# A hybrid encoder layer with a mixture of experts: the first expert's rows by one-hot products, unread products beside the router, and the mix's slot later in the ring

## The chip, the cores and the metric

The kernel runs on one core of a Trainium2 chip. The metric is the device time of one execution in microseconds (us). The kernel before takes 1461.59 us, the median of three runs (1460.72 to 1464.11). The profiled execution took 1457.25 us; its span, from the first instruction to the last, is 1455.5 us.

Engines are named as in the profile: PE multiplies matrices (PEld loads its weights), DVE is the vector engine, ACT the scalar engine, POOL the general one; SP issues most of the transfers. A queue's own row (SPq, POOLq) is the instruction that issues or waits.

## The reference, cut to what matters

A sequence of 512 tokens of width 1024 goes through one layer. A gated linear recurrence and a sparse attention each give half of the mix; then the top 4 of 32 experts work on each token.

```
h  = rms_norm(x) * (1 + sc1) + sh1;  z = h @ w_in
y_rnn  = rg_lru(...)                      # 512 columns
y_attn = dsa_attention(q, k, v, ...)      # 8 heads of 64
mix = concat(rms_norm(y_rnn), rms_norm(y_attn)) @ w_out
x   = x + g1 * mix
h2  = rms_norm(x) * (1 + sc2) + sh2
logits = h2 @ w_router + b_router;  gates = softmax(top 4)
for each expert e, on the tokens that chose it:
    u   = h2[tok] @ w1[e] + b1[e]         # 1024 x 2048
    act = clamped_swiglu(u)
    y  += gate * (act @ w2[e] + b2[e])    # 1024 x 1024
out = x + g2 * y
```

All is fp32. The expert weights alone are 32 times 12 MB.

## The kernel before, in words

The tokens lie in four tiles of 128 (index `i`). After the input products and the recurrence the kernel forms the mix, `part` (four tiles of 1024 in SBUF at `R[6]`), which starts as x. `rg_out_half(i, n, ...)` (twelve products of 512 columns, written out by `mm3`) adds the recurrent half of the mix for one tile and one half of the columns; `mix_half` does so for the attention's half. Before, all eight `rg_out_half` are handed to `attend` in a list; `attend(i, between)` takes one of them after every second head. A scheduler then orders each engine's instructions by its own estimate of when they are ready, so an engine's order is not the program's; `order` rows below show it.

`norm_heads` and `prep_q` ready q for the heads. `router_tile(i)` transposes a finished tile of the mix, forms the router's logits, picks four experts (`selb`, 1 where chosen; `gts`, the gates), builds h2 for the tile and writes it to `h2_d` in HBM.

The experts come as places in a list: `ORDER` gives the number of 32-row blocks of each (`NBS`: 3, 3, then 4, 2, 3, 2, 3 five times, and 4, 2, 1, 2, 1). The first two places are experts 0 and 1, fixed; the other thirty are ranked by their number of rows (`rank_experts`). `places` computes for every token and expert the position among that expert's rows (`pos`); `route` turns positions into row numbers (`idx_all`) and gates by one-hot products; `gather` fetches the rows of h2 from HBM by an indirect DMA on POOL; `turn_x` transposes them on PE into `xTs`. Then `up` (8 weight blocks of 1 MB), `glu`, `turn_act`, `down` (4 blocks of 1 MB) and `add_out` (an indirect DMA that adds to the output). PE does up(j), then the transposes for j+1, then down(j-1). After the first `up`, `gated_bias` adds the experts' bias to `part` and writes it to the output as the base of the sums.

Weights arrive through a ring of nine slots of 16 KB per partition, two loads of 1 MB in each. `wslot` takes the slots in the order of `slots_at` and issues the two loads on SP, which works in order: a load that must wait for its slot holds up all later ones. The places `R[0]` to `R[6]` (16 KB each) and those at 148 and 164 have earlier uses, and a slot's first load waits for these: R1, weights of the recurrent half; 148 and 164, k and q; R2, R5, weights of the attention's half; R4, y; R3 and R0, work space of the router; R6, the mix, which is free only when `gated_bias` has written it out.

```
for j in range(E + 1):
    ...
        w = load_up(w1_of(expert(j)));  up(j, w, nb);  glu(j, nb)
        turn_x(j + 1, ...);  bias(j + 1, ...)
    if j == 0: gated_bias()
    if j: down(load_down(w2_of(expert(j - 1))), ...);  add_out(j - 1, ...)
```

Of the kernel before, what the change touches and what calls it, by code (L numbers as in the profile page):

```python
# [13 lines left out]
OP = mybir.AluOpType  # L14
# [5 lines left out]
NT = S // 128  # L20
KD = D // 128
# [16 lines left out]
def layer(ctx, tc, x, c, w_ada, b_ada, norm1_g, w_in, conv_w, conv_b, w_rg_a, b_rg_a, w_rg_x, b_rg_x,  # L38
# [74 lines left out]
    A2r, sh2r = [mem(R[3] + 8 + 4 * j, D) for j in range(2)]  # L113
# [432 lines left out]
    load_wo(1)  # L546
    rq = norm_heads(zq, "q", 191.5, [mem(174.75 + 2 * j, S) for j in range(2)])
# [77 lines left out]

    def router_tile(i):
        o = part[:, i]
        x2T, h2 = [mem(R[0] + 8 * j + 4 * (i % 2), D) for j in range(2)]
        x2T = x2T.rearrange("p (k t) -> p k t", k=KD)
        for q in range(2):  # L630
            p = bank(4, 5)
            for k in range(4):
                T.transpose(p[:, k * 128:(k + 1) * 128], o[:, 4 * q + k::KD], ident)
            A.copy(x2T[:, 4 * q:4 * q + 4, :], p.rearrange("p (k t) -> p k t", k=4))
        ss2 = const.tile([128, 1], F32, name="ss2", tag="ss2", bufs=2)
# [32 lines left out]
    rg = [partial(rg_out_half, i, n, *half_a) for i in (3, 2, 1, 0) for n in range(2)]  # L668
    attend(3, rg[0:4])
# [17 lines left out]
    attend(2, rg[4:6] + [partial(mix_half, 3, n, *m3, *half_b) for n in range(2)])  # L687
    m2 = mix_in(2)
    attend(1, rg[6:8] + [partial(mix_half, 2, n, *m2, *half_b) for n in range(2)])
# [35 lines left out]
    slots_at = (164, 148, R[1], R[4], R[2], R[5], R[0], R[3], R[6])  # L725
# [91 lines left out]
    def wslot(blocks, n, src):  # L817
        nslot[0] += 1
        kb = slots_at[(nslot[0] - 1) % len(slots_at)]
        t = [mem(kb + 8 * j, blocks, n) for j in range(2)]  # L820
        for j in range(2):
            nc.sync.dma_start(t[j], src(j))
        return t
# [33 lines left out]
    def turn_x(j, frm, nb):  # L857
        n = BT * (4 if nb == 3 else nb)
        for q in range(2):
            p = bank(4, 5).rearrange("p (k t) -> p k t", k=4)  # L860
            for k in range(4):
                T.transpose(p[:, k, 0:n], xgs[frm][0:n, 4 * q + k::KD], ident[0:n, 0:n])  # L862
            (V.tensor_copy if q else A.copy)(xTs[j % 2][:, 4 * q:4 * q + 4, 0:n], p[:, :, 0:n])  # L863

# [70 lines left out]
    def gated_bias():  # L935


        g2r = mem(120, D)
# [24 lines left out]
    xg_of = lambda j: 2 - j if j < 2 else (j - 2) % 3  # L963
    places(selb, gts, 0, 2)
    route(0, 2)
    gather(0, xg_of(0), NBS[0])
    gather(1, xg_of(1), NBS[1])
    turn_x(0, xg_of(0), NBS[0])
    bias(0, bias_col(0))
# [115 lines left out]
```

## Time and profile before

| what | value |
|---|---|
| median of three runs | 1461.59 us |
| profiled execution | 1457.25 us |
| its span | 1455.5 us |
| PE busy | 1352.9 us, 93% of the span |
| DVE, ACT, POOL busy | 543.0, 273.8, 204.0 us |
| weight loads of the experts | 384 of 1024 KB, 15.8 us from issue to landing (median) |
| HBM read | 465.14 MB, 330 GB/s over the span |

Up to about 390 us the kernel works on the mix and the router, from there on the experts. The page cuts the span in 40 slices of 36.4 us; a digit is the busy share of a slice in tenths. PEclk or "clock" is the granted clock of PE as a share of 2.4 GHz: 1.00 is 2.4 GHz, 0.50 is 1.2 GHz. An fp32 product shows as two records, and four products of 32 weight columns run side by side on four parts of the array.

### The profile page before, as it was taken

Reading aid. Unit: us, or ns where it says so; the run is one execution under the profiler, and the core shown is the slowest. Engines: PE = TensorE matmul, PEld = TensorE weight load, DVE = VectorE, ACT = ScalarE, POOL = GpSimd, SP = SyncE. Lnnn points to the kernel's source line nnn. Section 1 sums busy time; section 2 is a strip of 40 time slices with the busy share of each in tenths; the row PEclk is TensorE's granted clock in tenths of the full one; section 3 lists DMA queues with packets and bytes.
Section 4 is the critical chain, followed back from the end, with each engine's and each line's share of the span. In section 5 each row is a group of like instructions: output and inputs, shape, how many; then the busy total and the mean of one; then the engine's idle time right before and its main releaser. Section 6 shows DMA issues by size and latency. Waiting matters only on the chain. (4 is left out here: it accounts for less than half of the span.)

```text
span 1455.5 us, 26508 instructions
## 1 busy us (share of the span) xinstructions
PE 1352.9 (93%) x10907; PEld 599.8 (41%) x10907; DVE 543.0 (37%) x1317; ACT 273.8 (19%) x552; POOL 204.0 (14%) x238
## 2 busy tenths in 40 slices
PE   5999996999599999999999999999999999999984
PEld 2854875778333343433333333333333333333220
DVE  4579896657532213213222321223132122212221
ACT  4454553434101101101010000001010010100100
POOL 4412623601100000000000010000000000100000
PEclk9999998899699999999999999999999999999996
DMA  9776113015869999999999999999999999999994
GB/s 377 227 267 224 59 58 117 22 44 220 346 249 409 411 399 402 395 399 414 399 407 397 425 403 385 412 407 378 411 399 405 406 406 408 390 398 383 395 417 188
DMA packets 83399, 482.40 MB, mean 331 GB/s; under 512 B 11778, under 2 KB 14018, under 8 KB 33098
## 3 DMA queue, kind: packets, MB, share of 16 engines
q1 hardware_dynamic: 75034, 453.88, 77.5%
q0 software_dynamic: 7520, 24.68, 6.7%
q8 instruction: 88, 1.44, 0.4%
q10 hardware_dynamic: 720, 2.10, 0.4%
q14 instruction: 37, 0.30, 0.1%
HBM read 465.14 MB, written 15.48 MB: 330 GB/s over the span
## 5 line engine op out<-in xcount | busy, mean ns | idle before, releaser
L883 PE MATMUL bank<-mem,mem 128*32 128x512 f32 x5504 | 621.4, 594 | 0.0
L883 PEld LDWEIGHTS bank<-mem,mem 128*32 128x32 f32 x5504 | 174.6, 110 | 369.4 <-issue 359.0
L910 PE MATMUL bank<-mem,mem 128*32 128x512 f32 x2304 | 268.3, 593 | 0.8 <-DMA mem<-in_w_dram 0.8
L888 DVE TENSOR_TENSOR bank<-bank,mem 128x512 f32<-128x512 f32 x86 | 60.0, 697 | 413.3 <-PE bank L883 413.2
L910 PEld LDWEIGHTS bank<-mem,mem 128*32 128x32 f32 x2304 | 82.4, 110 | 149.6 <-issue 136.3
L890 ACT ACTIVATE mem<-bank 128x256 f32<-128x256 f32 x86 | 33.1, 385 | 535.3 <-DVE bank L888 535.3
L932 POOL DMA_INDIRECT out_dram<-mem,idx_all x32 | 47.0, 1469 | 604.3 <-DVE mem L929 570.7
L929 DVE SCALAR_TENSOR_TENSOR mem<-bank,gate_h,mem 64x512 f32<-64x512 f32 x72 | 53.9, 749 | 203.2 <-PE bank L910 202.5
L157 PE MATMUL bank<-mem,mem 128*128 128x512 f32 (+1 forms) x320 | 114.1, 358 | 0.6 <-ACT mem L293 0.2
L158 PE MATMUL bank<-mem,mem 128*128 128x512 f32 (+1 forms) x320 | 112.0, 350 | 0.0
L159 PE MATMUL bank<-mem,mem 128*128 128x512 f32 (+1 forms) x320 | 111.6, 349 | 0.0
L854 POOL DMA_INDIRECT mem<-h_d,idx_all x32 | 30.1, 941 | 385.8 <-PE bank L862 328.0
L916 PE MATMUL bank<-mem,mem 128*32 128x512 f32 x448 | 62.9, 614 | 4.6 <-SPq L1014 2.9
L157 PEld LDWEIGHTS bank<-mem,mem 128*128 128x128 f32 x320 | 61.6, 193 | 13.0 <-issue 5.0
L159 PEld LDWEIGHTS bank<-mem,mem 128*128 128x128 f32 x320 | 61.7, 193 | 10.4 <-issue 4.7
L158 PEld LDWEIGHTS bank<-mem,mem 128*128 128x128 f32 x320 | 61.8, 193 | 10.0 <-issue 4.4
L862 PE MATMUL bank<-ident,mem 128*128 128x128 f32 (+2 forms) x256 | 44.1, 296 | 20.1 <-DMA mem<-h_d,idx_all 10.8
L863 DVE COPY mem<-bank 128x512 f32<-128x512 f32 (+2 forms) x32 | 18.1, 564 | 119.7 <-PE bank L862 119.4
L862 PEld LDWEIGHTS bank<-ident,mem 128*128 128x128 f32 (+2 forms) x256 | 33.8, 196 | 67.8 <-issue 28.5
L901 ACT COPY mem<-bank 128x512 f32<-128x512 f32 (+1 forms) x32 | 18.3, 573 | 208.5 <-PE bank L910 123.1
L153 POOL TENSOR_TENSOR mem<-mem,mem 128x512 fp32r<-128x512 f32 (+1 forms) x28 | 41.3, 1490 | 84.3 <-ACT mem L152 84.2
L900 PEld LDWEIGHTS bank<-ident,mem 128*128 128x128 f32 x172 | 24.5, 207 | 37.4 <-issue 21.1
(325 smaller groups left out, 1192.8 us busy)
## 6 DMA issues: line engine op xcount, KB each, us to landing
mem<-in_w_dram SPq DMA_DIRECT2D x384, 1024.0 KB, 15.8
mem<-in_w_ada_dram SPq DMA_DIRECT2D x24, 1024.0 KB, 8.3
mem<-in_w_in_dram SPq DMA_DIRECT2D x20, 512.0 KB, 4.5
mem<-in_x_dram SPq DMA_DIRECT2D x8, 512.0 KB, 5.7
mem<-in_w_out_dram SPq DMA_DIRECT2D x8, 512.0 KB
mem<-in_w_in_dram SPq DMA_DIRECT2D x8, 256.0 KB, 6.2
mem<-mod_d SPq DMA_DIRECT2D x4, 512.0 KB
h_d<-mem POOLq DMA_DIRECT2D x4, 512.0 KB, 6.4
```

Source lines behind the costliest of these rows:

```text
L153: (sub or V).tensor_sub(lo, src, hi)
L157: T.matmul(p, ah, bh, start=(k == 0), stop=False)
L158: T.matmul(p, al, bh, start=False, stop=False)
L159: T.matmul(p, ah, bl, start=False, stop=(k == n - 1))
L862: T.transpose(p[:, k, 0:n], xgs[frm][0:n, 4 * q + k::KD], ident[0:n, 0:n])
L883: T.matmul(bk[b][32 * n:32 * n + 32, :], xT[:, k, BT * b:BT * b + BT], w[k][:, 0, n * 512:(n + 1) * 512], start=(k == 0), stop=(k == KD - 1))
L888: V.tensor_add(bk[b], bk[b], biasb[j % 2])
L890: A.activation(act[:, b], u[:, :, 0], AF.Gelu_apprx_sigmoid)
L910: T.matmul(bk[6 + b // 2][o:o + 32, :], aT[:, b, c, BT * n:BT * n + BT], w[n][:, c, m * 512:(m + 1) * 512], start=(n + c == 0), stop=(n == ...
L916: T.matmul(bk[6 + nb // 2][o:o + 32, :], aT[:, nb - 1, c, BT * n:BT * n + BT], w[n][:, c, m * 512:(m + 1) * 512], start=(n == 0), stop=(n ...
L929: V.scalar_tensor_tensor(ys[64 * h:64 * h + a.stop - a.start, ns], p[a], gate_h[a, h, j:j + 1], g2h[a], op0=OP.mult, op1=OP.mult)
L932: G.indirect_dma_start(out=out_rows, out_offset=bass.IndirectOffsetOnAxis(ap=idx_all[a, j:j + 1], axis=0), in_=ys[a], in_offset=None, comp ...
```

## The change

It has four parts. The first four of the eight `rg_out_half` are issued right after the loads of `w_out`, ahead of `norm_heads` for q; the other four stay with `attend`. `router_tile` puts h2 into four lasting places (`h2s`), and for tiles 1 and 0 a new helper `dense` issues three fp32 products of 512 columns whose result nobody reads; eight short bf16 ones stand ahead of `places`. The first expert's rows come from `select_x`: one-hot columns made of `pos` by DVE, and 32 fp32 products of h2 in SBUF with them, which give the rows already transposed. `gather(0)` and `turn_x(0)` are gone; `route(0, 2)` now follows. The ring's first round leaves out R6, which joins at the end of the second; the order of the other slots changes, and A2r, sh2r, the transposed tiles and g2r move to other places.

```diff
-    A2r, sh2r = [mem(R[3] + 8 + 4 * j, D) for j in range(2)]
+    A2r, sh2r = [mem(R[0] + 8 + 4 * j, D) for j in range(2)]
...
     load_wo(1)
+    rg = [partial(rg_out_half, i, n, *half_a) for i in (3, 2, 1, 0) for n in range(2)]
+    for f in rg[0:4]:
+        f()
...
+    h2s = [mem(kb, D) for kb in (120, 128, 144, R[0] + 4)]
+
+    def dense(a, b, n):
+        for j in range(n):
+            T.matmul(bk[1][:, 0:b.shape[1]], a, b, start=True, stop=True)
+
     def router_tile(i):
         o = part[:, i]
-        x2T, h2 = [mem(R[0] + 8 * j + 4 * (i % 2), D) for j in range(2)]
-        x2T = x2T.rearrange("p (k t) -> p k t", k=KD)
+        x2T, h2 = mem((116, 112, R[0], R[0])[i], KD, 128), h2s[i]
...
+        if i < 2:
+            dense(ident, x2T[:, 0:4].rearrange("p k t -> p (k t)"), 3)
...
-    attend(3, rg[0:4])
+    attend(3, rg[4:6])
...
-    attend(2, rg[4:6] + [partial(mix_half, 3, n, *m3, *half_b) for n in range(2)])
+    attend(2, rg[6:7] + [partial(mix_half, 3, n, *m3, *half_b) for n in range(2)])
...
-    attend(1, rg[6:8] + [partial(mix_half, 2, n, *m2, *half_b) for n in range(2)])
+    attend(1, rg[7:8] + [partial(mix_half, 2, n, *m2, *half_b) for n in range(2)])
...
-    slots_at = (164, 148, R[1], R[4], R[2], R[5], R[0], R[3], R[6])
+    slots_at = (R[1], 164, 148, R[4], R[3], R[2], R[5], R[0])
+    slot_of = lambda n: slots_at[n] if n < 8 else (slots_at + (R[6],))[(n - 8) % 9]
...
+    def select_x(n):
+        oh = mem(134.25, NT, n)
+        for i in range(NT):
+            V.tensor_scalar(oh[:, i], slots[:, 0:n], pos[:, i, 0:1], None, op0=OP.is_equal)
+        for q in range(2):
+            p = bank(4, 5).rearrange("p (k t) -> p k t", k=4)
+            for k in range(4):
+                for i in range(NT):
+                    T.matmul(p[:, k, 0:n], h2s[i][:, 4 * q + k::KD], oh[:, i], start=(i == 0), stop=(i == NT - 1))
+            (V.tensor_copy if q else A.copy)(xTs[0][:, 4 * q:4 * q + 4, 0:n], p[:, :, 0:n])
...
-        g2r = mem(120, D)
+        g2r = mem(116, D)
...
+    dense(onesb, selb.rearrange("p i e -> p (i e)"), 8)
     places(selb, gts, 0, 2)
+    select_x(BT * NBS[0])
+    bias(0, bias_col(0))
     route(0, 2)
-    gather(0, xg_of(0), NBS[0])
     gather(1, xg_of(1), NBS[1])
-    turn_x(0, xg_of(0), NBS[0])
-    bias(0, bias_col(0))
```

The scheduler's result, at three places. First SP, before: the loads around the ring's second round. mem_3219 and mem_3220 are the two loads of the slot at 164, mem_3223 and mem_3224 those at 148, mem_3227 the first of R1, mem_134 and mem_135 those of R6; "waits" names the queues and engines whose signal the row needs.

```order
L822 DMA mem_3219<-in_w_dram 128x2048 [waits DMAHW0_49,PE_49]
L822 DMA mem_3220<-in_w_dram 128x2048 [waits DMAHW1_49,PE_49]
...
L822 DMA mem_3223<-in_w_dram 128x2048 [waits DMAHW3_49,PE_49]
...
L822 DMA mem_3224<-in_w_dram 128x2048 [waits DMAHW6_49,PE_49]
...
L822 DMA mem_3227<-in_w_dram 128x2048 [waits DMAHW0_49,PE_49]
L822 DMA mem_134<-in_w_dram 128x2048 [waits DMAHW4_49,DMAHW5_49,DMAHW2_49,DMAHW7_49,DMAHW1_49,DVE_49]
L822 DMA mem_135<-in_w_dram 128x2048
```

Now, from the load of g2r (L962) to the second round; mem_76 is in R3, mem_3470 in R2, mem_132 and mem_133 in R5, mem_3476 and mem_3477 in R0, mem_3259 and mem_3260 in R1, mem_3263 at 164:

```order
L833 DMA mem_79<-in_w_dram 128x2048 [waits DMAHW7_49,PE_49,Activation_49]
L962 DMA mem_2891<-mod_d 128x1024 [waits DMAHW0_49,PE_49,Activation_49]
L833 DMA mem_76<-in_w_dram 128x2048 [waits DMAHW1_49,DVE_49,Pool_49]
L833 DMA mem_3470<-in_w_dram 128x2048 [waits DMAHW2_49]
...
L833 DMA mem_3476<-in_w_dram 128x2048 [waits DMASW5_49,DMAHW6_49,PE_49,Pool_49]
L833 DMA mem_3477<-in_w_dram 128x2048 [waits DMAHW7_49,DVE_49,Pool_49]
L833 DMA mem_3259<-in_w_dram 128x2048 [waits DMAHW0_49,PE_49]
L833 DMA mem_3260<-in_w_dram 128x2048 [waits DMAHW1_49,PE_49]
L833 DMA mem_3263<-in_w_dram 128x2048 [waits DMAHW2_49,PE_49]
```

Before, R6 is the 22nd load; now it is the 33rd, and the load of g2r, which had its place free, waits for PE and ACT ahead of the loads of R3, R2, R5 and R0.

Second PE, now, from the router's last tile to the places; L642 are transposes, L650 the router's products, L634 the unread ones (before, the rows are the same without L634):

```order
L642 MATMUL bank_69<-ident,mem_103 128x128 x4
L634 MATMUL bank_66<-mem_2835,ident 128x512 [waits DVE_49]
L634 MATMUL bank_66<-mem_2835,ident 128x512 x2
L650 MATMUL bank_68<-mem_82,mem_2835 128x32 [waits Activation_49]
...
L642 MATMUL bank_69<-ident,mem_103 128x128 x4
L634 MATMUL bank_66<-mem_2891,ident 128x512 [waits Activation_49]
L634 MATMUL bank_66<-mem_2891,ident 128x512 x2
L650 MATMUL bank_65<-mem_82,mem_2891 128x32 x4
```

The unread products stand between a tile's transposes and its router products, on the same queue.

Third PE, now, ahead of the first head; L475 are q's transposes, bank_67 with L157 and L158 is the fifth half tile, L576 and L577 the first head:

```order
L159 MATMUL bank_68<-mem_188,mem_1192 128x512
L475 MATMUL bank_70<-ident,mem_76 128x128 [waits DVE_49]
...
L475 MATMUL bank_69<-ident,mem_76 128x128 x4
L157 MATMUL bank_67<-mem_1652,mem_1192 128x512 [waits DVE_49]
L158 MATMUL bank_67<-mem_1652,mem_1193 128x512
...
L576 MATMUL bank_65<-mem_92,mem_94 128x512 [waits DVE_49]
L577 MATMUL bank_65<-mem_93,mem_94 128x512
```

Before, one half tile stood ahead of L475 and the first head followed it at once; now four stand ahead of it, and the beginning of a fifth between L475 and the first head.

## Rows read from the trace of the kernel before

**Rows 1.** The page's busy tenths in 40 slices: PE and DMA.
```profile
PE   5999996999599999999999999999999999999984
...
DMA  9776113015869999999999999999999999999994
```

**Rows 2.** Stretches: length, engines' busy us and counts, then PEclk, DMA share, GB/s.
```profile
260.00:264.00 4.00, 4.00 (x10) 3.12 (x10) 3.61 (x7) 3.48 (x9) 1.28 (x1) 0.50 0.34 98
...
370.00:375.00 5.00, 1.46 (x32) 0.97 (x31) 4.42 (x21) 0.71 (x3) 2.33 (x2) 0.54 1.03 434
...
415.00:420.00 5.00, 5.00 (x43) 2.16 (x36) 2.66 (x5) 1.30 (x4) 0.00 (x0) 1.00 0.30 123
...
430.00:435.00 5.00, 5.00 (x49) 1.81 (x49) 1.12 (x9) 0.00 (x0) 0.91 (x1) 1.00 0.70 222
...
440.00:445.00 5.00, 5.00 (x52) 1.56 (x48) 0.00 (x0) 0.00 (x0) 0.00 (x0) 1.00 1.02 433
```

**Rows 3.** Waits of SP's queue: us in total, times, longest us.
```profile
SPq L822 <- DMA out_dram<-mem: 20.6, 3, 18.1
```

**Rows 4.** Timeline of SP's queue, 357 to 435 us: start, duration, instruction.
```profile
357.22 0.65 SPq L939 DMA_DIRECT2D mem<-mod_d  x1
362.58 2.76 SPq L822 DMA_DIRECT2D mem<-in_w_dram  x4
...
400.71 0.33 SPq L822 DMA_DIRECT2D mem<-in_w_dram  x1
...
411.01 0.33 SPq L822 DMA_DIRECT2D mem<-in_w_dram  x1
432.15 2.88 SPq L822 DMA_DIRECT2D mem<-in_w_dram  x3
```

**Rows 5.** A stretch of ten microseconds at 1230 us, columns as in rows 2.
```profile
1230.00:1240.00 10.00, 9.13 (x68) 3.19 (x60) 3.56 (x15) 0.70 (x2) 1.73 (x2) 1.00 1.02 420
```

**Rows 6.** Timeline of PE, 367 to 427 us; in brackets idle before and releaser.
```profile
367.13 2.05 PE L639 MATMUL bank<-mem,mem 128*128 128x32 f32 x16 [0.28 <-ACT mem L634]
373.28 0.16 PE L766 MATMUL bank<-selb,later 128*128 128x2 bf16 x1 [4.11 <-DVE selb L651]
...
392.26 1.97 PE L862 MATMUL bank<-ident,mem 128*128 128x128 f32 x8 [10.76 <-DMA mem<-h_d,idx_all]
394.17 0.62 PE L869 MATMUL bank<-b1t,foldb 96*32 96x512 bf16 x4
...
399.60 19.08 PE L883 MATMUL bank<-mem,mem 128*32 128x512 f32 x174
418.62 1.17 PE L862 MATMUL bank<-ident,mem 128*128 128x128 f32 x8
...
426.90 1.06 PE L883 MATMUL bank<-mem,mem 128*32 128x512 f32 x6
```

**Rows 7.** Timeline of POOL, 373 to 384 us.
```profile
373.39 0.57 POOL L659 DMA_DIRECT2D h_d<-mem  x1 [1.17 <-DVE selb L651]
...
383.05 1.00 POOL L854 DMA_INDIRECT mem<-h_d,idx_all  x1 [5.32 <-DVE pos L774]
```

**Rows 8.** Timeline of DVE, at the first head and at the router.
```profile
252.70 0.75 DVE L522 SCALAR_TENSOR_TENSOR mem<-bank,rs,mem 128x512 f32<-128x512 f32 x1
...
370.99 1.26 DVE L647 TENSOR_SCALAR m8r<-m8r 128x4 f32<-128x4 f32 x1
...
374.87 0.16 DVE L774 TENSOR_TENSOR pos<-mem,mem 128x8 f32<-128x8 f32 x1
```

**Rows 9.** Timeline of PE ahead of and in the attention, 235 to 270 us.
```profile
235.60 0.40 PE L158 MATMUL bank<-mem,mem 128*128 128x512 f32 x1
...
237.89 0.39 PE L159 MATMUL bank<-mem,mem 128*128 128x512 f32 x1
247.21 0.47 PE L475 MATMUL bank<-ident,mem 128*128 128x128 f32 x1 [8.93 <-DVE mem L550]
...
269.06 1.00 PE L566 MATMUL bank<-mem,mem 128*128 128x64 f32 x8
```

More of the change, by code (lines that the diff above doesn't have):

```diff
@@ L667, in layer @@
     V.tensor_sub(upto_me, onesb, later)
-    rg = [partial(rg_out_half, i, n, *half_a) for i in (3, 2, 1, 0) for n in range(2)]
-    attend(3, rg[0:4])
+    attend(3, rg[4:6])
     half_b = split_out(1, R[5], gat)
@@ L818, in wslot @@
         nslot[0] += 1
-        kb = slots_at[(nslot[0] - 1) % len(slots_at)]
+        kb = slot_of(nslot[0] - 1)
         t = [mem(kb + 8 * j, blocks, n) for j in range(2)]
```

## The prediction, made before the result was known

> **What bounds the kernel now.** I read the page's forty slices first. PE stands at 9 nearly everywhere, and from the thirteenth slice on (440 us) so does the share of the DMA engines [rows 1]. A full PE row proves little, since a product counts as busy up to an end that is only modelled. Its counts are the better witness: at 1230 us PE starts 68 records in ten microseconds, busy 9.13, while DMA stands at 1.02 [rows 5]; at 440 us it has 52 in five [rows 2]. So from 440 us on the 384 weight loads of 1 MB set the end, and PE now and then waits for one. An earlier end must come from DMA time that is lost ahead of 440 us.
>
> Trainium Kernel Development and Optimization (the Trainium skill, section Performance Expectations) calls matmul busy time a bad metric in the same way. By PE's busy row the experts would be PE's, which is the first rival below; the trace's 68 records speak for the rule.
>
> That loss shows in five-microsecond stretches: DMA is at 0.30 at 415 and 0.70 at 430 [rows 2]. The SP queue's waits name it: 18.1 us in one piece for the writes to the output [rows 3]. In SP's timeline a load goes out at 400.71 (the 17th), the next ones 2.58 us apart until 411.01 (the 21st), and then none until 432.15 [rows 4]. The 22nd goes to slot R6, which holds the mix until that is written out, and all later loads stand behind it. The 17th itself waits for PE: it needs the slot of the first expert's first weight block, and PE reaches that expert only after 10.76 us of idling for its gathered rows [rows 6]. POOL can send that gather only at 383.05, though the last rows of h2 went out at 373.39 [rows 7].
>
> **The change part by part.** All times are of the profiled execution: span 1455.5, 1457.25 in all, 4.3 below the median 1461.59 of the timed runs. I sum differences and set the sum against the median.
>
> *Products of the first half of the mix, moved ahead.* PE has 8.93 us of idle time before 247.21 [rows 9]. A half tile is twelve products whose starts stand 0.229 us apart (235.60 to 237.89 in ten steps), so 2.74 us. Before, one half lies ahead of the gap, now four: three halves, 36 products, 8.2 us of PE work, leave the attention, where PE is full, for the gap. Against it: DVE adds four halves before it readies q for the first head, 0.75 each [rows 8], so three more make 2.3 us; and a fifth half stands ahead of the first head in PE's queue and waits for the bank that the first add frees. Bounds: +3 (the delay alone) to -11 (8.2, and half of the 6 us that the stretch at 1.2 GHz around 260 [rows 2] costs). I take 8.2 - 2.3 and a little for a half that ran at 1.2 GHz there: -6.5.
>
> *Unread products beside the router.* For tiles 1 and 0 three 512-column fp32 products go ahead of the router's own. The experts' products, four side by side, start 174 records in 19.08 us [rows 6], four in 0.44; a record that has the array to itself thus takes some 0.43, a product two records, three products 2.6 us. Tile 0's router products then end near 373.6 instead of 369.2 (16 records in 2.05 from 367.13). Part of it is given back: DVE now does tile 0's h2 ahead of the logits, where before it stood in between, and a 4-column operation took 1.26 us beside POOL's add [rows 8]. PE's wait for the selection, 4.11 [rows 6], should fall to about 1.5, six small operations. So the places start at 375.1 instead of 373.28; the eight short bf16 products ahead of them take about 0.55 more. Bounds: 0 (all of it inside the wait) to +5 (at 1.2 GHz).
>
> *Selecting rows instead of gathering them.* Gone from the path: the wait until 383.05, the gather (landing at 392.26), eight transposes (1.97). Added: four comparisons on DVE, the first about 0.3, behind pos, which ended 1.75 us after the places began (374.87 + 0.16 [rows 8]); and 32 fp32 products, 64 records of 128x128 weights and 96 columns. The trace has no such shape. The nearest are the attention's 64-column values, 8 records in 1.00 [rows 9], and the router's 32-column products, 16 in 2.05 [rows 6]: both 0.12 to 0.13 a record at 2.4 GHz whatever the columns. I take 0.12, 7.7 us. The other bound is eight transposes in 1.97 at 1.2 GHz [rows 6], 0.24 a record, 15.4 us. The clock fell in this place before (0.54 at 370 [rows 2]), and some 4 us of thin work remain between the unread products and the selection, so I add 2.3 for a start at 1.2 GHz. Behind the selection in PE's queue stand the bias (0.62 [rows 6]) and the ranking and route products, which lay beside the gather before; I take about three times the bias for them, 2.0, so 2.6 in all. First weight block done: 375.1 + 0.55 + 1.75 + 0.3 + 7.7 + 2.3 + 2.6 + 2.6 (the block) = 392.9; with the attention's 6.5 386.4, 14.3 earlier than 400.71.
>
> TensorE: Matmul & The Clock Gate (the Trainium skill, section LDWEIGHTS) prices a weight load by its columns alone, 128 of them at an estimated 0.107 us. No run here shows it at 96 columns; the router's 0.128 is a fifth above it. By the page's price the 64 records take 6.8 us, and if neither clock mattered to them the sum would be 3.2 better. That is part of the second rival.
>
> *The ring.* R6 leaves the first round. Loads 17 to 32 go to the eight other slots, R6 takes 33 and 34, when the mix is long out. Load 22 then follows five steps of 2.58 behind load 17: 386.4 + 12.9 = 399.3 instead of 432.15, 33 us earlier. Not all of that stays. After load 24 the ring is full; load 25 needs a block of the second expert, which PE begins only after the mix's last products (418.62 to 426.90, 8.3 us [rows 6]). DMA stands for those 8.3, and some 2 more at the first four-block expert, whose blocks take 4/3 of 2.58, 3.44 each. Kept: 33 - 10.3 = 22.5. The load of g2r now goes where tile 0's transposed rows lie and waits for their last reader (about 373), where before it went out at 357.22; behind it on SP stand R3, R2, R5 and R0, which before went from 362.58 [rows 4]. I cost that at nothing: these are the second expert's blocks, needed some 30 us later, and at 2.6 us each all sixteen are in by 392. If they come slower, up to 4 us.
>
> **Sum.** -22.5: span 1433, profiled 1434.8, median 1439.
>
> **Rivals.**
> First, PE and not DMA bounds the experts once the ring is full. For it: a three-block expert takes PE 2.58 a load, nearly what a load takes. Against: 1230 us [rows 5]. Then R6 gives nothing of its own, and only the first expert's end counts: 418.62 to about 405, -13.6: 1448.
> Second, the clock holds: no fall behind 250, none before the selection. For it: PE's idle pieces are a third of the old ones. Against: thin work remains in both places. Another 4.5 in the attention and 2.3 at the selection: 1432.
> Third, the selection runs at 1.2 GHz throughout, DMA still the bound. For it: the clock was at half in this place before, 0.54 on average from 370 [rows 2]. Against: the records come without a pause. 7.7 - 2.3 = 5.4 lost: 1444.5.
> Fourth, slower: PE's order. Unread products, selection, ranking and route all stand ahead of the first weight block on an engine that takes them in turn. At 1.2 GHz the selection costs 5.4 more and the unread products 5; if the attention hangs on DVE and gives +3, the first block ends at 392.9 + 5.4 + 5 + 3 = 406, and if PE bounds, 5.6 are lost: 1467. It decides once the first block ends after 400.71 and PE bounds; with DMA as the bound the ring alone keeps the kernel faster.
> That R6's wait merely comes later I hold for unlikely: the mix was out by 432, and load 33 is due behind 435.
>
> **How the numbers follow.** Forecast 0.38 (1434 to 1443), first rival 0.25, second 0.13, third 0.10, fourth 0.08, and 0.06 for the middle between first and fourth, no change. A measurement of this kernel can tell about 0.2% (2.9 us) from none. Faster 0.86, same 0.06, slower 0.08. Below 1430 lies half of the second, above 1453 the fourth, the middle and a little of the first: range 1430 to 1453.
>
> **What would show it.** SP's waits hold no 18 us for the output, and load 22 goes out near 399; the hole in DMA between 411 and 432 becomes one of about 8 us beside the mix's last products. The selection is 64 records in 7.7 us at a clock near 1, or 15 at 0.5. The first block ends near 386. The last mix product ends some 6.5 earlier. Wrong, if DMA stands below 0.95 for long stretches after 440 (then PE bounds), or the first block ends after 395.

## The result, and the profile after

The changed kernel is slower: 1472.59 us, the median of nine runs (1463.93 to 1475.76), against 1460.72 us for the kernel before, measured beside it (1458.82 to 1464.11). The ratio is 1.0079, 95% interval [1.0063, 1.0095]. The forecast was 1439.0 us, in 1430 to 1453. The ratios below all compare with the kernel before on the same chip; they weigh all undisturbed runs and need not equal the quotient of two medians.

The profiled execution took 1475.06 us, span 1473.3. That is 17.8 more than the span before, of which some 6 are chance: this execution lies 2.5 above its median, that of before 3.5 (to 1460.72) below. The page's tenths for PE, the granted clock and DMA:

```profile
PE   5999988999999999999999999999999999999984
...
PEclk9999998986789999999999999999999999999996
DMA  9676113034689999999999999999999999999994
```

PE is no emptier than in [rows 1], but its clock dips in slices 7 and 9 to 12. From slice 13 on PE's two rows look alike. So most of the loss is made ahead of 440 us. Five stations of the two executions, read from the timelines of PE, DVE and SP, say where:

| us | before | after | later by |
|---|---|---|---|
| end of the mix's last product | 363.92 | 375.04 | 11.1 |
| selb of the last tile | 373.23 | 385.84 | 12.6 |
| first record of up(0) | 394.57 | 405.09 | 10.5 |
| 192nd (last) record of up(0) | 418.09 | 436.15 | 18.1 |
| 35th weight load goes out | 454.4 | 472.5 | 18.1 |
| span | 1455.5 | 1473.3 | 17.8 |

The mix is 11.1 late, the selection takes nearly as long as the gather's way did (19.3 from selb to up(0), 21.3 before), and up(0) takes 7.5 more. Nothing is gained behind. Part of the 11.1 is chance: in eleven profiled executions of kernels with all eight halves in attend the mix ends anywhere from 363.9 to 374.3, and that of before is the earliest of the eleven. In PE's timeline of the changed kernel the selection is L885, up(0) L906; the ranking's and the routing's short products stand between (those of L776 to L780 are left out):

```profile
385.89 0.61 PE L634 MATMUL bank<-selb,onesb 128*128 128x128 bf16 x8 [1.30 <-DVE selb L662]
...
388.49 15.54 PE L885 MATMUL bank<-mem,mem 128*128 128x96 f32 x64 [0.62 <-DVE mem L880]
403.96 0.62 PE L892 MATMUL bank<-b1t,foldb 96*32 96x512 bf16 x4
404.50 0.65 PE L817 MATMUL bank<-perm,mem 32*128 32x32 f32 x8
405.09 1.92 PE L906 MATMUL bank<-mem,mem 128*32 128x512 f32 x2
406.93 0.38 PE L848 MATMUL bank<-pay,mem 128*128 128x5 bf16 x8
...
408.02 1.94 PE L906 MATMUL bank<-mem,mem 128*32 128x512 f32 x8
...
411.38 3.64 PE L906 MATMUL bank<-mem,mem 128*32 128x512 f32 x10
```

In [rows 6] the gather's wait of 10.76 us stood here, the ranking lay inside it, and up(0) then ran 174 records in one piece. Now the selection's 64 records take 15.54, and the ranking cuts up(0) into pieces. The clock in longer stretches (columns as in [rows 2]), first before, then after:

```profile
290.00:310.00 20.00, 19.53 (x107) 14.72 (x106) 9.56 (x30) 5.58 (x15) 1.24 (x2) 1.00 0.00 1
333.00:348.00 15.00, 15.00 (x86) 12.79 (x86) 10.19 (x52) 6.06 (x20) 2.90 (x3) 0.89 0.20 81
357.00:372.00 15.00, 11.25 (x69) 9.69 (x69) 9.81 (x49) 4.52 (x13) 2.11 (x2) 0.95 1.01 401
385.00:405.00 20.00, 12.73 (x94) 4.96 (x98) 3.90 (x17) 2.46 (x3) 1.27 (x2) 0.68 0.75 254
405.00:420.00 15.00, 15.00 (x135) 5.15 (x128) 2.66 (x5) 1.30 (x4) 0.00 (x0) 1.00 0.75 284
```

```profile
290.00:310.00 20.00, 16.29 (x58) 11.96 (x57) 9.54 (x19) 3.58 (x10) 5.77 (x5) 0.66 0.00 1
333.00:348.00 15.00, 15.00 (x65) 13.31 (x65) 6.04 (x36) 5.33 (x17) 0.00 (x0) 0.54 0.10 39
357.00:372.00 15.00, 14.33 (x57) 12.34 (x58) 8.77 (x51) 4.80 (x12) 3.49 (x3) 0.54 1.01 368
385.00:405.00 20.00, 18.23 (x116) 17.26 (x115) 7.06 (x37) 1.75 (x6) 1.16 (x1) 0.59 0.82 314
405.00:420.00 15.00, 15.00 (x96) 4.80 (x99) 7.12 (x43) 1.50 (x2) 1.00 (x1) 0.63 0.54 187
```

The attention and the router lose their clock in three stretches where before had it. At 388.73, 0.24 us into the selection, it falls to 0.50 and stays there until 416.04, through the whole selection and the first part of up(0):

```profile
388.73:416.04 27.31, 27.31 (x139) 19.35 (x139) 9.29 (x45) 2.35 (x3) 2.16 (x2) 0.50 0.71 284
```

At 333 PE reads "15.00 busy" in both: with 65 records instead of 86 that is the same busy row for less work.

The SP queue shows what the ring's part did: of 18.1 us of waiting for the output [rows 3] 9.3 are left.

```profile
SPq L962 <- PE bank L650: 19.4, 1, 19.4
...
SPq L833 <- DMA out_dram<-mem: 9.3, 1, 9.3
```

Load 22 goes out at 431.6, not 18 us behind the 21st any more. But the wait is not gone: it stands at load 25 now (24 out at 436.8, 25 at 449.5), whose slot is not the mix's. And the load of g2r waits 19.4 us, up to 384.65, with loads 10 to 16 behind it. No PE row names a wait for a load between 400 and 480 us, so neither is seen to cost time there. Now SP's queue in a stretch of seven loads some 50 us later, each with what it waits for in that stretch, first before, then after:

```profile
466.65 20.93 SPq L822 DMA_DIRECT2D mem<-in_w_dram  x7
```

```profile
SPq L822 <- PE bank L883: 20.0, 7, 3.3
```

```profile
484.71 20.93 SPq L833 DMA_DIRECT2D mem<-in_w_dram  x7
```

```profile
SPq L833 <- PE bank L906: 20.6, 7, 3.9
```

Seven loads in 20.93 us in both, 3.43 apart, 18.06 later in the second. A load of a four-block expert costs PE 32 records, 3.44 us at four in 0.43; DMA needs 2.5 for a load, 1.05 MB at the 420 GB/s of [rows 5]. SP waits for PE's products in nearly all of the 20.93 us: the loads wait for PE here, at a DMA share of 1.02 and 1.01 in the two stretches.

### The profile page after: what moved, and what is told of

It reads as the page before. It is cut to its first block, busy times and chain, and to the rows that moved or that the text cites. A ratio compares the mean times of both kernels' runs of the same rounds, so it can differ in the third digit from the quotient of the medians.

```text
span 1473.3 us, 26646 instructions
## 1 busy us (share of the span) xinstructions
PE 1386.7 (94%) x10983; PEld 627.7 (43%) x10983; DVE 548.0 (37%) x1321; ACT 273.2 (19%) x552; POOL 204.3 (14%) x237
## 5 line engine op out<-in xcount | busy, mean ns | idle before, releaser
L906 PE MATMUL bank<-mem,mem 128*32 128x512 f32 x5504 | 628.1, 597 | 4.1 <-DMA mem<-in_w_dram 4.1
L906 PEld LDWEIGHTS bank<-mem,mem 128*32 128x32 f32 x5504 | 174.6, 110 | 376.0 <-issue 358.7
L157 PE MATMUL bank<-mem,mem 128*128 128x512 f32 (+1 forms) x320 | 115.5, 363 | 2.1 <-DVE mem L522 1.7
L158 PE MATMUL bank<-mem,mem 128*128 128x512 f32 (+1 forms) x320 | 114.0, 356 | 0.0
L159 PE MATMUL bank<-mem,mem 128*128 128x512 f32 (+1 forms) x320 | 113.0, 353 | 0.0
L157 PEld LDWEIGHTS bank<-mem,mem 128*128 128x128 f32 x320 | 62.6, 197 | 13.8 <-issue 3.5
L159 PEld LDWEIGHTS bank<-mem,mem 128*128 128x128 f32 x320 | 62.8, 196 | 12.9 <-issue 6.8
L158 PEld LDWEIGHTS bank<-mem,mem 128*128 128x128 f32 x320 | 62.9, 197 | 9.4 <-issue 3.5
L923 PEld LDWEIGHTS bank<-ident,mem 128*128 128x128 f32 x172 | 24.4, 207 | 40.1 <-issue 24.6
## 6 DMA issues: line engine op xcount, KB each, us to landing
mem<-in_w_dram SPq DMA_DIRECT2D x384, 1024.0 KB, 17.8
```

What stands on the lines that cost most here:

```text
L157: T.matmul(p, ah, bh, start=(k == 0), stop=False)
L158: T.matmul(p, al, bh, start=False, stop=False)
L159: T.matmul(p, ah, bl, start=False, stop=(k == n - 1))
L906: T.matmul(bk[b][32 * n:32 * n + 32, :], xT[:, k, BT * b:BT * b + BT], w[k][:, 0, n * 512:(n + 1) * 512], start=(k == 0), stop=(k == KD - 1))
```

## The experiments

**Part by part.** The first four kernels undo or do one part each.

e1, the kernel before with the early halves:

```diff
+    rg = [partial(rg_out_half, ...) ...]
+    for f in rg[0:4]: f()
-    attend(3, rg[0:4])
+    attend(3, rg[4:6])
```

> The kernel before with one part of the change alone: four of the eight rg_out_half ahead of norm_heads, two handed to attend(3), one each to attend(2) and attend(1). Theory A (the moved products were what kept PE full between the last heads and beside the router; without them PE thins out there, its clock falls to 1.2 GHz in two or three more stretches of some 14 us, and the mix ends later): last product of the mix near 374 instead of 363.8, about 10 us slower than before, 1471. Rival B (the attention is as quick or quicker, the loss of the changed kernel lies in the selection and in PE's order behind the router): mix ends at 357 to 364, 1455 to 1461.

Measured 1461.98 (1458.33 to 1468.23), ratio 1.0016 [1.0002, 1.0031]. Neither theory: the profiled execution (1468.23) ends its mix at 377.6, as A has it, but it is the slowest of twelve. The times go with the mean clock: five lie at 1458.3 to 1460.1 with 0.968 to 0.970, three at 1465.2 to 1468.2 with 0.962 to 0.964, four between. Two stretches of the profiled one:

```profile
290.00:310.00 20.00, 16.50 (x53) 12.36 (x53) 9.60 (x18) 3.31 (x9) 6.48 (x5) 0.58 0.00 1
333.00:348.00 15.00, 14.93 (x75) 13.25 (x75) 7.66 (x47) 6.61 (x22) 1.37 (x2) 0.65 0.09 38
```

That early halves alone bring these low stretches in some executions and not in others fits the two ends of these times, but only the profiled one shows its clock by stretches. On the median they cost 0.16%.

e2, the kernel before with the ring's part:

```diff
-    slots_at = (164, 148, R[1], R[4], R[2], R[5], R[0], R[3], R[6])
+    slots_at = (164, 148, R[1], R[4], R[2], R[5], R[0], R[3])
+    slot_of = lambda n: slots_at[n] if n < 8 else (slots_at + (R[6],))[(n - 8) % 9]
```

> The kernel before with the ring's part alone: R6 left out of the first round, joining at the end of the second; the other slots in the order of before. Theory A (from the second expert on to some 570 us the loads go out at PE's pace, so PE sets the end there and the stall of load 22 is covered): the 18 us wait for the output goes, and the time stays within 3 us of before, 1458 to 1463. Rival B (the prediction's step: DMA sets the end from 440 us on): some 20 us faster, about 1440.

Measured 1459.45, ratio 1.0009 [0.9995, 1.0023]. Theory A by its time, but its condition is not met: SP still waits for the output, now at load 23, which goes out at 432.4:

```profile
SPq L823 <- DMA out_dram<-mem: 14.1, 1, 14.1
```

So the edit moves the wait by one load and shortens it by 4.0 us, and tests less than it was meant to. Load 22 went out at 417.4 instead of 432.2, and load 35 at 458.2 instead of 454.4: 3.8 later, and so is the last record of up(0) in this execution (421.9 against 418.1). These loads went with PE, not with load 22. A ring without any such wait was not tried.

e3, the changed kernel with the halves back in attend (e1's edit the other way):

> The changed kernel with the eight rg_out_half given to attend as before; unread products, selection and ring stay. Theory A (as for the early halves on the kernel before): the mix ends near 364 instead of 374.6, and the end follows: about 11 us faster than the changed kernel, 1461. Rival B (the loss lies behind the router): within 4 us of the changed kernel, 1469 to 1475.

Measured 1469.86, ratio 1.0071 [1.0051, 1.0090]. Rival B: most of the loss stays. In the profiled execution the mix ends at 374.3 although the halves are late.

e4, the changed kernel with the gather back:

```diff
-    select_x(BT * NBS[0]);  bias(0, bias_col(0));  route(0, 2)
+    route(0, 2);  gather(0, xg_of(0), NBS[0])
     gather(1, xg_of(1), NBS[1])
+    turn_x(0, xg_of(0), NBS[0]);  bias(0, bias_col(0))
```

> The changed kernel with the first expert's rows by gather and transposes as before, into the buffer at 144; unread products, early halves and ring stay. Theory A (at 1.2 GHz the selection takes 15.2 us, as long as the gather's way: from selb to the first product of up(0) 20.5 us against 21.5): within 3 us of the changed kernel, 1470 to 1476. Rival B (the selection on PE, with ranking and route behind it, is the loss): 7 us or more faster, 1465 or less. Rival C (the selection at 1.2 GHz is still shorter): 4 us or more slower, 1477 or above.

Measured 1458.28 (1454.44 to 1465.70), ratio 1.0011 [0.9993, 1.0029]. Rival B. From selb to up(0) it is 19.8 us, as with the selection (19.3), but up(0) is 23.7 again instead of 31.1. So the selection costs not by being longer than the gather's way but by what stood in the gather's wait and now stands in up(0), and by the clock there.

e11, the kernel before with unread products in the gap ahead of the first head; the halves stay with attend:

```diff
     load_wo(1)
+    dense(10)              # fp32, 512 columns, unread
...
     for pr in range(4):
         prep_q(pr)
+        dense(2)
```

> The kernel before with ten unread fp32 products of 512 columns (20 records, 8.7 us) ahead of norm_heads and two after each prep_q; the rg_out_half stay with attend. Theory A (the stretch at 1.2 GHz from 240.7 to 264.6 costs the attention PE time): the clock stays at 1.00 or falls for less than 10 us, the mix ends 3 to 6 us earlier, 1455 to 1458. Rival B (PE waits for DVE's q there in any case): no earlier, 1459 to 1463.

Measured 1462.17, ratio 1.0007 [0.9993, 1.0021]: rival B. From 245 to 265 the clock is 0.83 instead of 0.51, and the mix ends at 367.9, no earlier than before's 363.9. Either the low stretch that the early halves shorten is hardly on the path (DVE's work on q is, by rival B), or the unread products cost what the clock gives back; which, was not tried.

**Who sets the pace of the experts.** e5 and e6 put ten unread fp32 products of 512 columns (20 records, 8.75 us by the trace) ahead of the products of one place of the kernel before:

```diff
+            if j == 4:      # e6: j == 28
+                for q in range(10):
+                    T.matmul(bk[1], ident, b2f[:, 0:512], start=True, stop=True)
             up(j, w, nb)
```

> The kernel before with ten fp32 products of 512 columns, unread, ahead of the products of the fifth place (about 510 us): 20 records of some 0.43, 8.7 us of PE time. Theory A (there the ring is full and SP's loads wait for PE, so PE sets the end): every later load goes out some 8.7 us later and most of it reaches the end, 1466 to 1469. Rival B (the prediction's step: DMA sets the end from 440 us on): hidden, 1459 to 1462.

> The same ten unread products ahead of the 29th place (about 1340 us) in the kernel before. Theory A' (late in the experts PE waits for loads, 18 to 19.5 of 20 us busy, so DMA sets the pace there): mostly hidden, 1460 to 1463. Rival B' (PE sets the pace to the end): 8.7 us longer, 1467 to 1469.

e5: 1463.70, ratio 1.0025 [1.0010, 1.0040]. e6: 1464.79, ratio 1.0037 [1.0021, 1.0052]. Neither pair of theories held as written: about 40 and 60% of the 8.75 us reach the end (by the intervals 1.5 to 5.8 and 3.1 to 7.6 us). When the loads go out, in us:

| load | before | after | e2 | e5 | e6 |
|---|---|---|---|---|---|
| 35 | 454.4 | 472.5 | 458.2 | 458.8 | 457.6 |
| 61 | 529.5 | 547.5 | 533.3 | 533.8 | 532.6 |
| 73 | 560.9 | 579.0 | 564.7 | 573.8 | 564.1 |
| 97 | 625.7 | 639.2 | 624.9 | 634.0 | 628.1 |
| 361 | 1366.0 | 1380.9 | 1368.2 | 1373.5 | 1376.4 |

In e5 load 73 is 8.6 later than load 61's offset would put it (12.9 against 4.3), load 97 still 4.0. So up to load 73 a delay of PE passes whole, and by load 97 about half of it is made up. There the kernel before is slow: its 24 loads from 73 to 97 take 64.8 us, and SP waits for earlier loads to land (first row, 561 to 626 us); in e2 they take 60.2, and it hardly does (second row, 565 to 625 us).

```profile
SPq L822 <- DMA mem<-in_w_dram: 39.1, 18, 3.8
```

```profile
SPq L823 <- DMA mem<-in_w_dram: 5.4, 8, 1.2
```

The other kernels with the old ring, e1, e6 and e11, take 63.4 to 64.0 there; the changed kernel, like e2, 60.2, so that its 18.1 at load 73 is 13.5 at load 97. So in this stretch the DMA does set the pace with the old ring, and the profiled executions with the new one gain some 4 us, which e2's median does not show at the end. (e18 below, with the mix's slot in the first round but the other slots in the new order, takes 60.1 too.) Neither engine sets the pace alone; early PE does.

**The ranking.** e7, the changed kernel with ranking, its places and route(2, 2) behind the products of up(0):

```diff
-    rank_experts();  places(sels, gtss, 2, E);  route(2, 2)
...
             up(j, w, nb)
+            if j == 0:
+                rank_experts();  places(sels, gtss, 2, E);  route(2, 2)
+                gather(2, xg_of(2), NBS[2])
```

> The changed kernel with the ranking, its places and the routing of places 2 and 3 moved behind the products of up(0). Theory A (these short products, which stood in the gather's wait before, cut up(0) in pieces and keep its clock low: up(0) took 31.1 us to its 192nd record against 23.5): up(0) takes 24 to 27 us; the ranking's chain on DVE then stands uncovered between up(0) and up(1), some 10 us, so the time is 1470 to 1480 all the same. Rival B (only the clock makes up(0) long, and it stays at 1.2 GHz for as long): up(0) still 29 us or more.

Measured 1475.89, ratio 1.0118 [1.0094, 1.0142]. Theory A, and more of it: up(0) takes 22.7 us, but the first record of down comes 49.8 behind it instead of 33.0, since the ranking's steps now stand bare between the two experts. The ranking needs a cover, and the gather's wait was one.

e8, gather and late halves; unread products, places of h2 and ring stay (the edits of e3 and e4):

> The changed kernel with both disputed parts undone: rows by gather and transposes, the eight rg_out_half as before; unread products, lasting h2 places and ring stay. Theory A (selection and early halves are the whole loss, ring and unread products are worth little): 1456 to 1461, without the times about 1465 that the run with early halves and gather had in 5 of 12. Rival B (ring or unread products cost something of their own): 1463 or more.

Measured 1461.39 (1456.22 to 1464.23), ratio 1.0009 [0.9995, 1.0024]: 0.4 us above theory A's range and below rival B's. The rest of the change is worth nothing that can be measured.

**The selection's records.** e9 keeps PE full up to the selection:

```diff
-    dense(onesb, selb.rearrange("p i e -> p (i e)"), 8)
+    dense(ident, h2s[0][:, 0:512], 4)
     places(selb, gts, 0, 2)
+    dense(ident, h2s[0][:, 512:1024], 4)
```

> The changed kernel with the eight short bf16 products ahead of places replaced by four unread fp32 products of 512 columns, and four more between places and the selection, to keep PE full up to the selection. Theory A (the clock is the selection's cost: it stands at 1.2 GHz through the 64 records and the first part of up(0) because PE thins out ahead of them): selection 7.7 to 8.5 us instead of 15.3, up(0) 26 to 28 us instead of 31, minus some 4 us for the unread products: 1463 to 1467. Rival B (records of 96 columns let the clock fall whatever stands ahead): selection 12 us or more, 1472 to 1477.

Measured 1470.66, ratio 1.0069 [1.0045, 1.0093]. Between the two ranges. The selection takes 15.34 us, as rival B has it, but for a reason that neither theory had, and up(0) 27.9, as theory A has it. PE's timeline, and the clock within the selection (columns of the last two rows: PE, PEld, clock, DMA share, GB/s of line 885 alone):

```profile
387.43 3.68 PE L634 MATMUL bank<-mem,ident 128*128 128x512 f32 x8
390.94 15.34 PE L885 MATMUL bank<-mem,mem 128*128 128x96 f32 x64
```

```profile
391.00:394.00 3.00, 3.00 (x14) 3.00 (x13) 1.00 1.03 434
395.00:398.00 3.00, 3.00 (x15) 3.00 (x14) 0.50 1.04 437
```

14 records touch three microseconds at a clock of 1.00, 15 at 0.50: 0.238 apart in both. The full clock does not shorten these records. It fell at 394.5, in the middle of 64 records that followed each other without a pause.

e10 swaps the operands: the one-hot columns are the weights, h2 moves in 512 columns, and the rows are transposed as a gather's. Its g2r lands in the place of the first expert's activations, so that expert's share is not the reference's; e13 has g2r at 116 and the rows at 140.

```diff
-                    T.matmul(p[:, k, 0:n], h2s[i][:, 4 * q + k::KD], oh[:, i], ...)
+                T.matmul(p[0:n], oh[:, i], h2s[i][:, q * 512:(q + 1) * 512], ...)
+    turn_x(0, ...)
```

> The changed kernel with the selection's operands swapped: the one-hot columns are the weights, h2 moves through in 512 columns (16 records instead of 64), the rows are copied to SBUF and transposed as a gather's would be; g2r at 140. At 1.2 GHz the 16 records take 13.7 us, at 2.4 GHz 6.9; the transposes 1 to 2. Theory A (the 96-column records are what leaves the clock low): the clock returns within the selection, up(0) starts 2 to 5 us earlier and is shorter, 1464 to 1469. Rival B (what follows the selection matters more, the ranking in up(0)): up(0) stays at 29 us or more, 1470 to 1475.

Measured 1462.49, ratio 0.9997 [0.9976, 1.0018]: theory A, more of it than expected.

> The changed kernel with the selection's operands swapped (one-hot columns as weights, h2 moving in 512 columns, 16 records), rows copied to SBUF at 140 and transposed 96 wide; everything else as in the changed kernel. Theory A (the selection's shape is the loss): 16 records in 7 to 9 us, the clock back at 1.00 before up(0), up(0) near 24 us instead of 31; 10 us faster than the changed kernel, 1460 to 1464, the kernel before again. Rival B (the rank's products inside up(0) are the loss): up(0) 28 us or more, 1468 or more.

Measured 1456.39 (1450.24 to 1463.93), ratio 0.9972 [0.9951, 0.9994]. Theory A, below its range, and faster than the kernel before. 16 records in 8.96 us to the end of the last, up(0) 24.4, though the ranking cuts it here too.

e12 leaves the operands and takes neighbouring columns of h2 as weights, on e9:

```diff
-    h2s[i][:, 4 * q + k::KD]
+    h2s[i][:, (4 * q + k) * 128:(4 * q + k + 1) * 128]
```

> The run with unread products up to the selection (e9), with the selection's weights taken as 128 neighbouring columns of h2 instead of every eighth: the first expert's features then come in another order than its weights, so its share of the output is not the reference's. In e9 the 64 records started 0.238 us apart at a granted clock of 1.00 (390.9 to 394.5) and at 0.50 alike. Theory A (weights read with a stride of eight bound the record): 0.12 to 0.19 us a record at 1.00, selection 8 to 13 us, 4 to 8 us faster than e9 (1470.7). Rival B (the stride is nothing; a two-record product with 128 weights and 96 columns takes that in any case): 15.3 us again, within 3 us of e9.

Measured 1460.69, ratio 0.9997 [0.9980, 1.0014], ten us below e9: theory A. Its timeline, and then line 885 (durations in ns: least, median, most) in e9 from 391 to 394 us, where the clock is 1.00, and in e12:

```profile
383.81 7.28 PE L885 MATMUL bank<-mem,mem 128*128 128x96 f32 x64
```

```profile
L885 PE MATMUL bank<-mem,mem x14: 246/401/403, 390.9 to 393.9; 128*128 128x96 f32 x14
L885 PEld LDWEIGHTS bank<-mem,mem x13: 313/335/338, 390.9 to 393.8; 128*128 128x128 f32 x13
```

```profile
L885 PEld LDWEIGHTS bank<-mem,mem x64: 190/192/192, 383.4 to 390.7; 128*128 128x128 f32 x64
L885 PE MATMUL bank<-mem,mem x64: 246/275/275, 383.8 to 390.8; 128*128 128x96 f32 x64
```

At full clock the weight load falls from 335 to 192 ns and the record from 0.238 to 0.111 us, by the stride of eight alone. The clock stays at 1.00 through selection and up(0):

```profile
384.00:387.00 3.00, 3.00 (x29) 3.00 (x28) 1.00 1.02 431
```

SBUF — State Buffer (the Trainium skill, section Door 1: The DMA port swizzle) says that successive reads within 16 bytes, four fp32, run at full rate and that each step to another such line is paid for. A step of eight fp32 is 32 bytes; the pair 0.238 and 0.111 at full clock agrees with the rule. The prediction did not weigh it; it spoke against this change.

**What the parts are worth with the selection mended.** e14 is e13 with late halves; e15 is e14 without the unread products.

> As e13, with the eight rg_out_half given to attend as before. Theory A (early halves are worth nothing on the median and bring times some 8 us longer in about half of the runs): 1458 to 1462, narrower than e13. Rival B (with the selection mended the early halves help): slower than e13 by 2 us or more.

> As e14, without the unread products beside the router and ahead of places. Theory A (they stand in PE's waits and give nothing): within 2 us of e14. Rival B (they hold the clock for the router and the selection): 3 us or more slower than e14, the selection's 16 records mostly at 1.2 GHz.

e14: 1455.69 (1453.69 to 1459.38), ratio 0.9969 [0.9956, 0.9982]. e15: 1456.39, ratio 0.9980 [0.9962, 0.9998]. e14 is below theory A's range, but as A has it no slower than e13 and narrower (5.7 us from the lowest to the highest run, e13 13.7); e15 is theory A. The selection's records take 8.96 us from the first start to the last in e15 and 8.37 in e14 (and in e13), and that is all the unread products are seen to give.

e16 stores h2 in blocks of every eighth feature, so that the selection reads neighbouring columns and its result is the reference's; e17 adds late halves, e18 R6 back in the ring's first round.

```diff
+            hq = h2.rearrange("p (k q) -> p q k", k=KD)[:, q * 64:(q + 1) * 64]
-            V.scalar_tensor_tensor(h2[:, ns], o[:, ns], r, A2r[:, ns], ...)
+            V.scalar_tensor_tensor(hq, turned(o), r, turned(A2r), ...)
```

> The changed kernel with h2 stored in blocks of every eighth feature (DVE and POOL write it so, h2_d holds it so, the transposes of the gathered rows read neighbouring columns too): the selection reads 128 neighbouring columns and gives the reference's output. Theory A (the stride of the weights is the whole of the selection's loss and of the clock behind it): 64 records in 7.1 us as in e12, no fall of the clock in up(0), 1453 to 1459, 14 us or more faster than the changed kernel. Rival B (the strided writes of h2 cost as much on DVE, ahead of the places): selb to the selection 2 us or more later, 1460 to 1466.

> As e16, with the eight rg_out_half given to attend as before. Theory A (the median changes little, the times above 1458 that early halves bring go): 1452 to 1456, the fastest of all. Rival B (early halves help once the selection is mended): slower than e16 by 2 us or more.

> As e17, with R6 in the ring's first round again (as its ninth slot). Theory A (PE sets the pace while the ring fills; the wait for the mix's slot is covered): within 2 us of e17. Rival B (with an earlier first expert the stall of that load reaches PE): 4 us or more slower than e17.

e16: 1459.27 (1450.98 to 1463.14), ratio 0.9994 [0.9973, 1.0015], 0.3 us above A's range and below B's; from selb to the selection it is 2.6 us as in the changed kernel, so the strided writes cost nothing there. e17: 1455.77 (1453.37 to 1458.97), ratio 0.9976 [0.9961, 0.9991], in A's range, though e18 is faster. e18: 1454.76, ratio 0.9968 [0.9952, 0.9985], theory A. SP's wait for the output is 15.4 us in e18, from load 24 on, and 8.9 in e17, at load 25, so these two differ in a part of the wait only. The profile of e16 is the cleanest pair to that of the changed kernel: its mix ends at 374.87 and its selb stands at 385.67, 0.17 from the other, and yet up(0) ends 11.8 earlier and the span is 1454.5, 18.8 less. The other 7.0 lie behind up(0), where executions differ by chance too: e3, with the changed kernel's code from there on, takes 1033.2 us from the last record of up(0) to the end, the changed kernel 1037.1.

```profile
388.31 8.98 PE L887 MATMUL bank<-mem,mem 128*128 128x96 f32 x64 [0.62 <-DVE mem L882]
...
397.91 1.04 PE L908 MATMUL bank<-mem,mem 128*32 128x512 f32 x2
...
409.29 15.65 PE L908 MATMUL bank<-mem,mem 128*32 128x512 f32 x142
```

```profile
385.00:405.00 20.00, 18.40 (x184) 13.41 (x187) 12.47 (x68) 3.25 (x7) 2.49 (x3) 0.91 0.99 376
405.00:420.00 15.00, 15.00 (x136) 4.65 (x132) 1.77 (x13) 0.00 (x0) 0.98 (x1) 1.00 1.01 397
```

The clock falls at 388.52 here too, 0.2 us into the selection, but it comes back at 391.93, within it. So e16 shows the records of neighbouring columns at both clocks (columns as for e9, line 887 alone):

```profile
388.60:391.60 3.00, 3.00 (x16) 3.00 (x15) 0.50 1.01 390
392.00:395.00 3.00, 3.00 (x29) 3.00 (x28) 1.00 1.00 418
```

They start 0.213 us apart at 0.50 (weight loads 333 ns) and 0.112 at 1.00 (192 ns). At half clock the stride thus adds little, 0.238 against 0.213; what it takes away is the gain from the full clock, and in this pair the clock's return within the selection. Four more profiles go the same way: in e3 and e7, with the stride, the clock stays at 0.50 to the selection's end and beyond, in e17 and e18, without it, it returns within the selection.

The ranking cuts up(0) here too, in the same pieces, and at 2.4 GHz it takes 26.4 us: 2.9 more than the 23.5 of before, whose up(0) began at 0.50 (until 397.75). The other 4.6 of the changed kernel's 31.1 are the clock. e13, e14, e15, e17 and e18 are faster than the kernel before, by 0.2 to 0.3%; the intervals do not tell them apart.

## Why the prediction was wrong, step by step

**"From 440 us on the 384 weight loads of 1 MB set the end."** Failed, and with it the largest term, 22.5 us. The DMA share of 1.02 and PE's 52 records in five microseconds were both read rightly, but neither says who waits. The queue does: up to load 73 the loads go out at PE's pace (seven in 20.93, SP waiting for PE in 20.0), and a full ring cannot be fuller. What the stall of load 22 cost SP was made up by load 35. In the changed kernel load 22 goes out no later than before, and yet load 35 is 18.1 late, as up(0) is. The step is right for a stretch behind load 73, where the old ring leaves the DMA behind; the 4 us or so gained there do not show in e2's median. The first rival had said "R6 gives nothing of its own", and e2, and e17 against e18, agree; but they only shorten the wait for the output, as the change itself does (9.3 us left), so what a ring without it gives is not shown. The rival's price of 1448 took the other steps as they stood, and they fell too.

**The selection at 0.12 a record, 7.7 us.** Failed. It is 0.238 and 15.5, the prediction's other bound and the third rival's. Their reason, the clock, holds in part: it stood at 0.50 through the whole selection, and at 0.50 records of neighbouring columns would also take 0.213 (e16). But e9 shows 0.238 at full clock too: the stride keeps the records there, and no term had it. The rows chosen as nearest (the attention's values, the router's products) matched in type and in the weights' size, but read their weights without a stride. With neighbouring columns at full clock the 0.12 is right: 0.111 in e12. The clock then did not come back before 416.04, in e16 at 391.93, and up(0) began at 1.2 GHz.

**"Behind the selection stand the bias, the ranking and the route products, 2.0."** Failed in kind. The work of these products was sized, not their spread: they come one by one as DVE's steps allow, and without the gather's wait each stops up(0). With the clock that makes 7.5 us, 2.9 of them at full clock (e16; 0.9 in e13, where more stands between selection and up(0)).

**The attention's -6.5.** Failed: the gain did not come. The gap ahead of the first head was filled and the low stretch there is shorter, but the products taken out of attend were missing later, and the clock fell at 293, 334 and 358 us: +11.1 in the profiled execution. The bound of +3 counted DVE's delay alone. How much of it is the early halves stays open: e1 puts 0.16% on them, the other four pairs with and without them 0.02 to 0.18%, always to their loss, and kernels with late halves also end their mix anywhere from 364 (before) to 374 us (e3), so a part is chance from execution to execution.

**The unread products.** About right: selb stands 10.8 behind the mix's end, before 9.3; the term had 1.8 by the places.

**The fourth rival,** slower by PE's order with PE as the bound, 1467 at a chance of 0.08, is what came, and 5.6 us more: the first expert's block ended after 400.71 and PE set the pace, its two conditions. It had the order right. That its sum came near is in part luck: of its pieces the selection's 5.4 came, the unread products' 5 did not, and up(0)'s 7.5 it did not have.

**What would show it wrong.** The sign given for a bound by PE was DMA below 0.95 for long after 440. In stretches of 20 us DMA stands at 0.97 or more from 460 to 1440 us, and PE sets the pace all the same up to load 73. That test was blind. The other sign, a first block that ends after 395, did show: load 17, which waits for it, goes out at 417.7.

## What to carry to other kernels

Ask a full ring who waits for whom: the spacing of its loads against PE's time for a block, not the share of a DMA engine that is never empty. Price a product by a row that agrees in the stride of its weights too. Before a wait is removed, list what runs inside it on the other engines; that work does not go with the wait.

## What was not expected of the hardware

- An fp32 record with 128x128 weights read at a stride of eight takes 0.238 us at 2.4 and at 1.2 GHz alike; with neighbouring columns 0.111 at 2.4 and 0.213 at 1.2 GHz (e12, e16). Transposes with the same stride of eight show it in their weight loads (median 196 ns in the changed kernel, 139 with neighbouring columns in e16) but hardly in their pace: eight in 1.16 and in 1.09 us.
- In e9 the clock fell in a row of 64 such records without a gap, with PE busy all the time and after 3.68 us of 512-column products; in e12 it stayed at 1.00 through the same 64 records without the stride. This is one execution of each; the changed kernel and e16 agree with it.
- The times of e13 fall in two groups with the mean clock (1450.2 to 1453.9 at 0.974 to 0.976, 1458.8 to 1463.9 at 0.966 to 0.969). The profiles of the nine kernels with early halves fall in two groups as well: in five the clock is low for 13.6 us or more in each of three stretches, near 293, 335 and 358 us, and the mix ends at 374.0 to 377.6; in four it is low for at most 6.9 us at each of the first two, and the mix ends at 366.9 to 370.0. What decides between them is open.
